# A planner of issue order is given a later landing time for the memory tokens of layer 0 and a longer duration for one product

## The chip, the cores and the metric

The kernel runs on one core of a Trainium2 chip. The metric is the device time of one execution, in microseconds (us). The core's engines run at the same time, each through its own queue in program order: PE (TensorE, matrix products and transposes), ACT (ScalarE), DVE (VectorE), POOL (GpSimd) and SP (SyncE, which here only issues DMAs).

## The reference

The reference is a decoder trunk of two layers on S = 256 tokens of width D = 1024, in float32. A layer runs three token-mixing branches on the same normed input, merges them, and then runs an MLP:

```
h = rmsnorm(x, ln_mix_pre[l])
xr, yr, q, kv, g_nsa, qm, g_merge = split(h @ w_in[l])
o_a = rglru_branch(xr, yr, ...)                # conv, gates, scan
o_b = nsa_branch(q, kv, g_nsa, positions, ...) # compressed, selected, window attention
o_c = memory_branch(qm, mem, ln_mem[l], w_mem_kv[l])  # rmsnorm(mem) @ w_kv, 4 heads
ga, gb, gc = split(sigmoid(g_merge))
merged = ga*(o_a @ w_br_rnn) + gb*(o_b @ w_br_nsa) + gc*(o_c @ w_br_mem)
x = x + rmsnorm(merged @ w_out[l], ln_mix_post[l])
h = rmsnorm(x, ln_mlp_pre[l])
x = x + rmsnorm(square(relu(h @ mlp_w1[l])) @ mlp_w2[l], ln_mlp_post[l])
```

The compressed part of `nsa_branch` (`compress`) builds overlapping blocks of 32 tokens from the keys and values, adds a position table, and sends them through a small MLP with a gelu.

## The kernel before

**Products.** Every weight matrix comes in units of 512 KB (usually two slices of 128 rows by 512 columns). SP loads a unit into one of five `raw` buffers (`dma_unit`, L336 to L343). ACT copies it to `whi` in the format that PE multiplies (a unit of 128x1024), and DVE subtracts to get the remainder `wlo` (`split_unit`, L345 to L364); there are four pairs of these. Activations are kept as such a pair too (`hTh` and `hTl`, and so on), and PE makes each product of three passes: high by high, high by low, low by high. A unit is 24 products of 256 columns, or 12 of 512.

**The order.** The issue order is not written by hand. While the program is built, `Meter` (L109 to L140) meets every call of an engine, works out a cost for it from the shapes, and advances a clock of that engine in `Order` (`od.T`, L78 to L93). Each strand of dependent work is a generator, a `Lane`, with `r`, the planned time at which its last result is there. `side` and `step` (L255 to L295) put the next piece of a lane into the order when its planned time has come on PE's planned clock. So a price in `Meter.call` or a planned landing does nothing on the chip by itself: it moves instructions ahead of others in the queues of PE, ACT, DVE and POOL, and where SP issues for a lane, in SP's. The chip then runs each queue in that order. In the profile all computing instructions carry the line of `Meter.call`, L140.

**The memory tokens.** `mem_prep` (L1751) loads the 256 memory tokens (four tiles of 128x512, L1760) behind the gains of their norm (L387), and spawns `norm_both`: for each of two token tiles, ACT squares and sums both halves (`junk<-mem`), POOL makes `rstd`, DVE scales each half (`hn<-mem,rstd,gain`), PE transposes it (`tr<-ident,hn`), and ACT and DVE copy it into the pair `mTh` and `mTl`. In `norm_both`, the first piece of each lane is allowed at `od.cur.r`, which `mem_prep` sets. For layer 0 it is called when the first job starts (`start`), for layer 1 at a later job. PE's first job in layer 0 is `xr1` and the second `xr0`, each 96 products of four units; units are counted here u0, u1, ... from the first.

**The compressed keys.** `kc_epi` (L1477) copies the product's result with ACT (`kcs<-mm`, two of them), and SP copies each of these with four DMAs into two shifted tiles (`g<-kcs`, L1489 and L1490). DVE then adds the position table (`gs<-g,pet`), ACT and DVE split the sum (`ghl`), and PE multiplies it (`hid`). Around it, ACT and DVE serve the recurrent branch: PE makes the gate products `gp`, ACT turns them into `ti`, `tr`, `aa`, `th`, and so on.

**The end of the mixing sub-layer.** `Residual` (L537) sums squares of the last product `wo`, adds the result to `x`, norms it and transposes it (`tr<-ident,hn`) for the MLP, one token tile after the other; products of `wo` for the second tile stand before and behind the first tile's transposes.

Of the kernel before, what the change touches and what calls it, by code (L numbers as in the profile page):

```python
# [11 lines left out]
F32 = mybir.dt.float32  # L12
# [86 lines left out]
def elems(ap):  # L99
    n = 1  # L100
    for d in ap.shape[1:]:
        n *= d
    return n


class Meter:
# [5 lines left out]
    def __getattr__(self, name):  # L112
        fn, key, order = getattr(self.eng, name), self.key, self.order

        def call(*args, **kw):
            out = kw["out"] if "out" in kw else args[0]
            n = elems(out)
            if key == "A":
                cost = 0.055 + n / 1200.0
                cost += 0.06 * sum(not isinstance(kw.get(k, 0.0), float) for k in ("scale", "bias"))  # L120
                cost += 0.12 if kw.get("accum_out") is not None else 0.0
                if args[2] in TABLES:
                    cost += 1.28 * (self.table != TABLES[args[2]])
                    self.table = TABLES[args[2]]
            elif key == "D":
                if "reduce" in name:
                    n = elems(args[1])
                cost = DCOST + n / (1920.0 if name == "tensor_scalar" else 960.0)
                cost += 0.06 * (name == "scalar_tensor_tensor")
            elif key == "P":  # L130
                if name == "transpose":
                    cost = 0.109
                else:
                    load = args[1].shape[1] / 1200.0
                    cost = max(load, 0.0025 + n / 2400.0) * (4 if args[1].dtype == F32 else 1)
            else:
                cost = 0.25
            aps = [v.tensor.name for v in (*args, *kw.values()) if hasattr(v, "tensor")]
            order.note(key, cost, out.tensor.name, aps if "out" in kw else aps[1:])
            return fn(*args, **kw)  # L140

        return call
# [3 lines left out]
def trunk_kernel(ctx, tc, x, mem, positions, ln_mix_pre, w_in, conv_w, conv_b, lru_wr, lru_br, lru_wi, lru_bi,  # L146
# [3 lines left out]
    od = Order()  # L150
# [22 lines left out]
    def a(shape, dt=F32, name="a"):  # L173
        return sp.tile(shape, dt, tag="a", bufs=NA, name=nm(name))
# [39 lines left out]
    def spawn(gen, name=None, prio=None, child=None):  # L214

        ln = Lane(gen, od.cur.r, od.cur.child if prio is None else prio)
        ln.child = child or od.cur.child
        ln.last = od.cur.last
        lanes.append(ln)
        lanes.sort(key=lambda v: v.prio)  # L220
        if name:
            named[name] = ln
        advance(ln)
        return ln
# [110 lines left out]
    dma_clock = [0.0]  # L335
# [47 lines left out]
    def gain_tile(g):  # L383
        res = []
        for h in range(2):
            gt = a([P, 512], F32, name="gain")
            nc.sync.dma_start(out=gt, in_=g[:, 512 * h:512 * h + 512].to_broadcast([P, 512]))  # L387
            res.append(gt)
        return res
# [126 lines left out]
    def norm_both(src, gt, o, name, prio=1):  # L516
        yield [spawn(norm_lane(src[t], t, gt, o, name), prio=prio) for t in range(NT)]
# [1235 lines left out]
    def mem_prep(l):  # L1753
        ms = []
        gm = gain_tile(ln_mem[l:l + 1, :])
        for t in range(NT):
            ms.append([])
            for h in range(2):
                m = a([P, 512], F32, "mem")
                nc.sync.dma_start(out=m, in_=mem[0, t * P:(t + 1) * P, 512 * h:512 * h + 512])  # L1760
                ms[t].append(m)
        env[l]["M"] = XT("mT")
        dma_clock[0] = max(dma_clock[0], od.T["D"] - 4.0) + 6 * 0.73
        od.cur.r = max(od.cur.r, dma_clock[0] + 2.0)
        spawn(norm_both(ms, gm, env[l]["M"], f"mnorm{l}"))

    def load_x(t):
# [9 lines left out]
    for l in range(DEPTH):  # L1777
        layer(l)
    jobs[0]["gb1"].pre = lambda: mem_prep(1)
    order = []  # L1780
    for l, names in enumerate((ORDER0, ORDER1)):
# [14 lines left out]
    def start():  # L1796
        first_pre()
        mem_prep(0)
        prows = load_params()
        load_consts()  # L1800
        od.cur.r = 26.0
        spawn(prm_lane(prows), "prm")
        od.cur.r = 36.0
        spawn(const_lane(), "const")
# [35 lines left out]
```

## Time and profile before

| | before |
|---|---|
| median of 3 runs | 1221.04 us (1216.6, 1221.04, 1221.95) |
| the profiled execution, its own time | 1221.59 us |
| its span in the trace | 1219.9 us |
| PE busy | 1199.6 us, 98% |
| DVE busy | 901.6 us, 74% |
| ACT busy | 736.7 us, 60% |
| POOL busy | 35.5 us, 3% |
| HBM traffic | 208.16 MB read, 172 GB/s over the span |

The profile is of one execution, 0.55 us above the median of the runs. The busy time of PE is that of pipelined instructions: a product of 256 columns is shown 0.28 us long while the next starts 0.12 us behind it, so gaps between starts say more than busy shares. The waits are rows of the timeline in which an idle time stands in brackets, with the engine and tile that ended it.

### The profile page before, as it was taken

The numbers are of one execution on the slowest core, as the hardware profiler recorded it, in microseconds if no ns is written. First come the engines' busy times: TensorE is split into PE (matmuls) and PEld (weight loads), VectorE is DVE, ScalarE is ACT, GpSimd is POOL, SyncE is SP. The second block draws the span as 40 slices with busy tenths as digits, with TensorE's granted clock in tenths as the row PEclk, the third lists the DMA queues.
The fourth block names the chain that finished last, engine by engine and source line by source line (L and its number), as shares of the span: only waits on it lengthen the run. The fifth ranks groups of instructions, "written<-read, shape, count | busy, mean of one in ns | idle before, by whom it ended". The sixth has DMA issues, their size and how long they took to land.

```text
span 1219.9 us, 19570 instructions
## 1 busy us (share of the span) xinstructions
PE 1199.6 (98%) x7371; PEld 1068.8 (88%) x7371; DVE 901.6 (74%) x1516; ACT 736.7 (60%) x1330; POOL 35.5 (3%) x88
## 2 busy tenths in 40 slices
PE   8899999999999999999999999999999999999997
PEld 7899988888888889998989999888888887899896
DVE  4778897979898686555557587998978877655555
ACT  4677856777666465445456688675656655645443
POOL 3000000000000020000001000000000001000000
PEclk9899999999999999999999999999999999999999
DMA  8555656753345666666656556584534356565561
GB/s 283 181 161 168 190 156 181 223 152 108 122 131 186 233 191 191 194 189 189 206 174 210 154 171 176 153 258 140 154 121 138 121 164 217 166 187 183 190 190 69
DMA packets 121263, 212.58 MB, mean 174 GB/s; under 512 B 10441, under 2 KB 24098, under 8 KB 121169
## 3 DMA queue, kind: packets, MB, share of 16 engines
q1 hardware_dynamic: 120752, 211.19, 55.9%
q8 instruction: 58, 0.95, 0.3%
q0 software_dynamic: 416, 0.15, 0.1%
q14 instruction: 37, 0.30, 0.1%
HBM read 208.16 MB, written 1.05 MB: 172 GB/s over the span
## 4 chain that ended last, share of the span: by engine, by line
PE 92%; DVE 2%; DMA 2%; ACT 2%; issue 1%; SPq 0%; POOL 0%; POOLq 0%; DVEq 0%; ACTq 0%
PE mm L140 62%; PE acc L140 14%; PE ob L140 2%; PE sc L140 2%; PE wo L140 2%; PE pt L140 2%; PE hid L140 1%; PE gp L140 1%; PE mo L140 1%; PE msc L140 1%; PE tr L140 1%; DMA mem<-in_mem_dram 1%; ACT junk L140 1%; DVE wlo L140 1%; DMA raw<-in_mlp_w_dram 1%
## 5 line engine op out<-in xcount | busy, mean ns | idle before, releaser
L140 DVE TENSOR_TENSOR wlo<-raw,whi 128x1024 fp32r<-128x1024 f32 (+1 forms) x371 | 447.1, 1214 | 225.7 <-ACT whi L140 224.3
L140 ACT ACTIVATE whi<-raw 128x1024 fp32r<-128x1024 f32 (+1 forms) x371 | 385.3, 1055 | 204.9 <-PE mm L140 117.0
L140 PE MATMUL mm<-hmh,whi 128*128 128x256 f32 x480 | 135.9, 283 | 0.0
L140 PE MATMUL mm<-hmh,wlo 128*128 128x256 f32 x480 | 135.9, 283 | 0.0
L140 PE MATMUL mm<-hml,whi 128*128 128x256 f32 x480 | 135.9, 283 | 0.0
L140 PE MATMUL mm<-hTh,whi 128*128 128x256 f32 x448 | 129.4, 289 | 0.0
L140 PE MATMUL mm<-whi,hTh 128*128 128x512 f32 x320 | 129.1, 403 | 0.0
L140 PE MATMUL mm<-hTh,wlo 128*128 128x256 f32 x448 | 127.6, 285 | 0.0
L140 PE MATMUL mm<-hTl,whi 128*128 128x256 f32 x448 | 127.6, 285 | 0.0
L140 PE MATMUL mm<-wlo,hTh 128*128 128x512 f32 x320 | 125.1, 391 | 0.0
L140 PE MATMUL mm<-whi,hTl 128*128 128x512 f32 x320 | 125.0, 391 | 0.0
L140 PE MATMUL acc<-whi,rh 128*128 128x512 f32 x256 | 99.8, 390 | 0.0
L140 PE MATMUL acc<-wlo,rh 128*128 128x512 f32 x256 | 99.8, 390 | 0.0
L140 PE MATMUL acc<-whi,rl 128*128 128x512 f32 x256 | 99.6, 389 | 0.0
L140 PEld LDWEIGHTS mm<-hmh,whi 128*128 128x128 f32 x480 | 92.1, 192 | 0.5
L140 PEld LDWEIGHTS mm<-hml,whi 128*128 128x128 f32 x480 | 92.1, 192 | 0.5
L140 PEld LDWEIGHTS mm<-hmh,wlo 128*128 128x128 f32 x480 | 92.1, 192 | 0.0
L140 PEld LDWEIGHTS mm<-hTh,whi 128*128 128x128 f32 x448 | 86.9, 194 | 0.2
L140 PEld LDWEIGHTS mm<-hTl,whi 128*128 128x128 f32 x448 | 86.9, 194 | 0.2
L140 PEld LDWEIGHTS mm<-hTh,wlo 128*128 128x128 f32 x448 | 86.7, 194 | 0.0
L140 PEld LDWEIGHTS mm<-whi,hTl 128*128 128x128 f32 x320 | 60.1, 188 | 13.1
L140 PEld LDWEIGHTS mm<-whi,hTh 128*128 128x128 f32 x320 | 60.2, 188 | 12.0 <-issue 0.2
(311 smaller groups left out, 2467.7 us busy)
## 6 DMA issues: line engine op xcount, KB each, us to landing
raw<-in_w_in_dram SPq DMA_DIRECT2D x136, 512.0 KB, 3.7
raw<-in_mlp_w_dram SPq DMA_DIRECT2D x128, 512.0 KB, 4.2
raw<-in_w_mem_kv_dram SPq DMA_DIRECT2D x32, 512.0 KB, 4.2
raw<-in_cmp_w_dram SPq DMA_DIRECT2D x16, 512.0 KB, 4.0
raw<-in_w_br_rnn_dram SPq DMA_DIRECT2D x16, 512.0 KB, 3.7
raw<-in_w_br_mem_dram SPq DMA_DIRECT2D x16, 512.0 KB, 3.7
raw<-in_w_br_nsa_dram SPq DMA_DIRECT2D x16, 512.0 KB, 3.7
raw<-in_w_out_dram SPq DMA_DIRECT2D x16, 512.0 KB, 4.5
```

The costliest lines, as they stand in the source:

```text
L140: return fn(*args, **kw)
```

## The change

Two expressions of the planner differ. In `Meter.call`, a product of n columns that is not plain float32 is priced at 0.0133 + n/2400 us instead of 0.0025 + n/2400: 0.120 us instead of 0.109 for 256 columns, and 0.227 instead of 0.216 for 512. A plain float32 product, of which there are few, is priced at four times 0.001 + n/2400. In `mem_prep`, the memory tokens of layer 0 are planned to land 12 us behind the planner's DMA clock instead of 2; for layer 1 it stays 2.

```diff
@@ -132,7 +132,7 @@
                     cost = 0.109
                 else:
                     load = args[1].shape[1] / 1200.0
-                    cost = max(load, 0.0025 + n / 2400.0) * (4 if args[1].dtype == F32 else 1)
+                    cost = (max(load, 0.0133 + n / 2400.0) if args[1].dtype != F32 else 4 * max(load, 0.001 + n / 2400.0))
             else:
                 cost = 0.25
@@ -1761,7 +1761,7 @@
         env[l]["M"] = XT("mT")
         dma_clock[0] = max(dma_clock[0], od.T["D"] - 4.0) + 6 * 0.73
-        od.cur.r = max(od.cur.r, dma_clock[0] + 2.0)
+        od.cur.r = max(od.cur.r, dma_clock[0] + (2.0 if l else 12.0))
         spawn(norm_both(ms, gm, env[l]["M"], f"mnorm{l}"))
```

PE's queue holds the same instructions as before, in another order. A few scalings and copies that either ACT or DVE may do go to the other of the two: ACT's queue has 15 instructions fewer and DVE's 15 more. SP's queue has one difference, in layer 0, where the eight DMAs of `g<-kcs` stand behind one more `raw`; POOL's is the same. Three places follow, with the names as the program numbers them.

**Place 1, layer 0, the memory tokens on PE.** Products of `xr0` around the first transposes; `whi_374` is u5, `whi_426` is u6 before, `whi_473` is u7 now, and `pet` is the transpose of the position table. Before, and now:

```order
L140 MATMUL mm_437<-hTh_114,whi_374 128x256
L140 MATMUL mm_437<-hTl_115,whi_374 128x256
L140 MATMUL mm_437<-hTh_114,wlo_375 128x256
L140 MATMUL tr_515<-ident,hn_456 128x128 x4
L140 MATMUL mm_436<-hTh_116,whi_426 128x256
```

```order
L140 MATMUL mm_417<-hTl_119,whi_473 128x256
L140 MATMUL mm_417<-hTh_118,wlo_474 128x256
L140 MATMUL pet_606<-ident,per_103 128x128
L140 MATMUL tr_621<-ident,hn_560 128x128 x4
L140 MATMUL tr_626<-ident,hn_562 128x128 x4
L140 MATMUL mm_646<-hTh_112,whi_512 128x256
```

The first transposes have moved from behind u5 to behind u7 and `pet`, 48 products later, and both halves of the first token tile now stand together; the second tile's two follow behind 12 products.

The same place on ACT, whose rows `junk<-mem` wait for the memory tokens; `raw_220` is u6, `raw_312` u7, `raw_318` u8. Before, and now:

```order
L140 ACTIVATE whi_374<-raw_214 128x1024
L140 ACTIVATE junk_392,ss_393<-mem_230 128x512
L140 ACTIVATE junk_395,ss_396<-mem_232 128x512
L140 ACTIVATE junk_398,ss_399<-mem_234 128x512
L140 ACTIVATE junk_401,ss_402<-mem_236 128x512
L140 ACTIVATE xs_416<-mm_263 128x512
L140 ACTIVATE xs_417<-mm_264 128x512
L140 ACTIVATE whi_426<-raw_220 128x1024
L140 ACTIVATE whi_485<-raw_312 128x1024
L140 ACTIVATE sp_476<-sp_475 128x16
L140 ACTIVATE whi_530<-raw_318 128x1024
```

```order
L140 ACTIVATE whi_374<-raw_214 128x1024
L140 ACTIVATE whi_406<-raw_220 128x1024
L140 ACTIVATE xs_404<-mm_263 128x512
L140 ACTIVATE xs_405<-mm_264 128x512
L140 ACTIVATE sp_450<-sp_449 128x16
L140 ACTIVATE whi_473<-raw_312 128x1024
L140 ACTIVATE whi_512<-raw_318 128x1024
L140 ACTIVATE junk_542,ss_543<-mem_230 128x512
L140 ACTIVATE junk_545,ss_546<-mem_232 128x512
L140 ACTIVATE junk_548,ss_549<-mem_234 128x512
L140 ACTIVATE junk_551,ss_552<-mem_236 128x512
L140 ACTIVATE whi_564<-raw_348 128x1024
```

The copies of u6, u7 and u8, and the two `xs`, stood behind the four rows of the memory tokens, and stand ahead of them now.

**Place 2, layer 1, the compressed keys.** ACT, from the gate product's `ti` on. Before, and now:

```order
L140 ACTIVATE ti_8284<-gp_8344,hb 128x256 x2
L140 ACTIVATE kcs_8360<-mm_8176 128x512
L140 ACTIVATE kcs_8361<-mm_8177 128x512
L140 ACTIVATE tr_8283<-gp_8364,hb 128x256 x2
L140 ACTIVATE aa_8285<-tr_8283,cc 128x256 x2
L140 ACTIVATE th_8286<-tr_8283,cc 128x256 x2
L140 ACTIVATE tr_8283<-aa_8285 128x512
L140 ACTIVATE ti_8323<-gp_8367,hb 128x256 x2
```

```order
L140 ACTIVATE ti_8254<-gp_8314,hb 128x256 x2
L140 ACTIVATE tr_8253<-gp_8332,hb 128x256 x2
L140 ACTIVATE aa_8255<-tr_8253,cc 128x256 x2
L140 ACTIVATE th_8256<-tr_8253,cc 128x256 x2
L140 ACTIVATE tr_8253<-aa_8255 128x512
L140 ACTIVATE ti_8293<-gp_8335,hb 128x256 x2
L140 ACTIVATE gelu_8195<-gelu_8195 128x512
L140 ACTIVATE whi_8349<-raw_8102 128x1024
L140 ACTIVATE kcs_8379<-mm_8222 128x512
L140 ACTIVATE kcs_8380<-mm_8223 128x512
L140 ACTIVATE whi_8399<-raw_8136 128x1024
```

The rows `kcs<-mm` stood right behind the first `ti`; now `tr`, `aa`, `th`, `tr`, the other `ti`, a gelu and a `whi` stand ahead of them. In PE's queue the `gp` products of that `tr` stand 24 products earlier than before, and the products of the next units where they stood.

DVE, from the end of the first group of `gs` to the second, which waits for the later four copies `g`. Before, and now:

```order
L140 TENSOR_TENSOR gs_8378<-g_1656_8373,pet 128x8x15
L140 TENSOR_TENSOR wlo_8436<-raw_8168,whi_8435 128x1024
L140 SCALAR_TENSOR_TENSOR gelu_8195<-gelu_8195,ys_8161 128x512
L140 MEMSET gs_8386 128x32
L140 TENSOR_TENSOR gs_8386<-g_1658_8380,pet 128x8x15
```

```order
L140 TENSOR_TENSOR gs_8388<-g_1656_8383,pet 128x8x15
L140 MEMSET gs_8396 128x32
L140 TENSOR_TENSOR gs_8396<-g_1658_8390,pet 128x8x15
L140 TENSOR_TENSOR gs_8396<-g_1659_8391,pet 128x8x15
L140 TENSOR_TENSOR gs_8396<-g_1658_8390,pet 128x8x15
L140 TENSOR_TENSOR gs_8396<-g_1659_8391,pet 128x8x15
L140 TENSOR_TENSOR wlo_8455<-raw_8214,whi_8454 128x1024
```

A `wlo` and a gelu stood between the two groups of `gs`; now both groups stand together, ahead of that `wlo`. Behind that `wlo` DVE's queue now holds `ghl`, `ti`, `th`, `wlo`, `ghl`, `gs`, `wlo`, as before in the same sequence; then `ghl`, `ml`, `ghl`, `ti`, two `xc`, a gelu and a `wlo`, where it had a `wlo` behind the first of its `ml`, `ghl`, `ti` and `th`.

**Place 3, layer 1, the transposes behind `wo` on PE.** Before, and now:

```order
L140 MATMUL wo_11286<-we_11376,mgl_11169 128x512
L140 MATMUL wo_11286<-we_11377,mgh_11168 128x512
L140 MATMUL wo_11286<-we_11379,mgh_11168 128x512
L140 MATMUL wo_11286<-we_11377,mgl_11169 128x512
L140 MATMUL tr_11522<-ident,hn_11512 128x128 x4
L140 MATMUL tr_11527<-ident,hn_11514 128x128 x4
L140 MATMUL wo_11287<-we_11392,mgh_11168 128x512
```

```order
L140 MATMUL wo_11286<-we_11376,mgh_11168 128x512
L140 MATMUL wo_11286<-we_11378,mgh_11168 128x512
L140 MATMUL wo_11286<-we_11376,mgl_11169 128x512
L140 MATMUL tr_11519<-ident,hn_11512 128x128 x4
L140 MATMUL tr_11524<-ident,hn_11514 128x128 x4
L140 MATMUL wo_11286<-we_11377,mgh_11168 128x512
L140 MATMUL wo_11286<-we_11379,mgh_11168 128x512
```

The two transposes of the first token tile stand three products of 512 columns earlier.

## Rows read from the trace of the kernel before

**Rows 1.** The page, busy time of the engines: share of the span, instructions.
```profile
PE 1199.6 (98%) x7371; PEld 1068.8 (88%) x7371; DVE 901.6 (74%) x1516; ACT 736.7 (60%) x1330; POOL 35.5 (3%) x88
```

**Rows 2.** Timeline of PE: start, duration, instruction, in brackets the idle time before.
```profile
31.53 0.28 PE L140 MATMUL mm<-hTh,wlo 128*128 128x256 f32 x1
34.97 1.12 PE L140 MATMUL tr<-ident,hn 128*128 128x128 f32 x4 [3.16 <-DVE hn L140]
...
41.26 0.28 PE L140 MATMUL mm<-hTh,wlo 128*128 128x256 f32 x1
41.38 1.04 PE L140 MATMUL tr<-ident,hn 128*128 128x128 f32 x8
42.17 0.36 PE L140 MATMUL mm<-hTh,whi 128*128 128x256 f32 x1
```

**Rows 3.** Table by stretch: busy of each engine, granted clock, DMA share, GB/s.
```profile
35.00:40.60 5.60, 5.60 (x27) 5.60 (x28) 5.39 (x14) 2.36 (x6) 0.00 (x0) 0.50 0.93 272
...
1026.00:1029.00 3.00, 1.36 (x8) 0.86 (x7) 1.23 (x3) 1.57 (x6) 1.76 (x4) 1.00 0.82 279
```

**Rows 4.** Timeline of ACT around the memory tokens.
```profile
28.34 0.63 ACT L140 ACTIVATE junk<-mem 128x512 bf16<-128x512 f32 x1 [7.17 <-DMA mem<-in_mem_dram]
...
29.01 0.63 ACT L140 ACTIVATE junk<-mem 128x512 bf16<-128x512 f32 x1
...
31.95 2.00 ACT L140 ACTIVATE whi<-raw 128x1024 fp32r<-128x1024 f32 x2
```

**Rows 5.** Timeline of POOL there, the first tile's `rstd`.
```profile
30.15 0.57 POOL L140 TENSOR_TENSOR rstd<-var,mhalf 128x1 f32<-128x1 f32 x1
```

**Rows 6.** The load of u8: its issue, and the time to its landing.
```profile
L341 SPq DMA_DIRECT2D raw<-in_w_in_dram x1: 379/379/379, 24.6 to 24.6; - x1
...
DMA to landing us min/median/max: 8.4/8.4/8.4
```

**Rows 7.** Timeline of ACT in layer 1.
```profile
740.88 1.30 ACT L140 ACTIVATE kcs<-mm 128x512 f32<-128x512 f32 x2
742.45 0.84 ACT L140 ACTIVATE tr<-gp,hb 128x256 f32<-128x256 f32 x2 [0.27 <-PE gp L140]
...
747.05 2.00 ACT L140 ACTIVATE whi<-raw 128x1024 fp32r<-128x1024 f32 x2
```

**Rows 8.** Timeline of SP there, the last issue of the compressed keys.
```profile
746.02 0.62 SPq L1490 DMA_DIRECT2D g<-kcs  x1
```

**Rows 9.** Tile g in layer 1: time from issue to landing.
```profile
DMA to landing us min/median/max: 3.0/3.5/3.9
```

**Rows 10.** Timeline of DVE in layer 1.
```profile
754.84 0.42 DVE L140 TENSOR_TENSOR ghl<-gs,ghl 128x256 fp32r<-128x256 f32 x1
...
758.13 0.90 DVE L140 TENSOR_TENSOR gs<-g,pet 128x120 f32<-128x120 f32 x3
758.95 1.22 DVE L140 TENSOR_TENSOR wlo<-raw,whi 128x1024 fp32r<-128x1024 f32 x1
760.08 0.68 DVE L140 TENSOR_TENSOR ml<-mm,mh 128x512 fp32r<-128x512 f32 x1
...
769.58 0.69 DVE L140 SCALAR_TENSOR_TENSOR ti<-th,ti 128x512 f32<-128x512 f32 x1
...
772.22 1.22 DVE L140 TENSOR_TENSOR wlo<-raw,whi 128x1024 fp32r<-128x1024 f32 x1
```

**Rows 11.** Timeline of PE, where it first reads the `wlo` behind the second group.
```profile
752.85 0.28 PE L140 MATMUL mm<-hTh,wlo 128*128 128x256 f32 x1
```

**Rows 12.** Timeline of PE around the first tile's transposes behind wo, layer 1.
```profile
1026.23 0.62 PE L140 MATMUL wo<-we,mgh 128*128 128x512 f32 x2
1026.68 0.39 PE L140 MATMUL wo<-we,mgl 128*128 128x512 f32 x1
1028.71 1.32 PE L140 MATMUL tr<-ident,hn 128*128 128x128 f32 x8 [1.64 <-DVE hn L140]
```

**Rows 13.** Waits of PE from 45 us on: for whom, total, times, longest.
```profile
PE gn L140 <- DVE wlo L140: 0.9, 1, 0.9
```

## The prediction

> **What bounds the kernel now.** The page's first part comes first: PE is busy for 1199.6 us [rows 1], so time is gained or lost only where PE stands or runs slowly. Hence I read PE's timeline for starts that lie further apart than the pitch, 0.12 us for a product of 256 columns (41.26 to 41.38), 0.225 for one of 512 (two in 0.45 us), 0.10 for a transpose (eight in 0.79) [rows 2, 12], and looked up what each gap waited for.
>
> The largest is the memory tokens' in layer 0. ACT stood 7.17 us for them until 28.34, with the copy of u6 queued behind: that starts at 31.95 [rows 4]. DVE has u6's `wlo` in its queue ahead of `hn`, so the first transposes, which wait for `hn`, start at 34.97, 3.3 us after PE was done with the product of 31.53 [rows 2]. Then PE runs at a granted clock of 0.50, the 1.2 GHz level, from 35.0 to 40.6 [rows 3]. In all, 31.53 to 42.17 is 10.64 us [rows 2] for 25 products and 16 transposes, 25 x 0.12 + 16 x 0.10 = 4.6. The price of this stall is **6.0 us**: 3.3 standing and 2.7 of slow clock.
>
> A shorter wait shows no such tail: before the transposes behind `wo` in layer 1 PE stood from 1026.9 to 1028.71 [rows 12], and the granted clock of that stretch is 1.00 [rows 3].
>
> **Part 1: the memory tokens (the later landing).** The transposes come 48 products and `pet` later in PE's queue: 31.65 + 48 x 0.12 + 0.1 = 37.5. Are they ready? On ACT the copies of u6, u7 and u8 now stand ahead of `junk<-mem`. u8 was issued at 24.6 and took 8.4 us to land [rows 6]: 33.0, when the tokens have landed, since ACT's rows for them ran on from 28.34 [rows 4]. Its copy takes about 0.95 (the second of a pair that starts at 31.95 and is 2.00 long [rows 4]), so `junk` starts at 33.95. Its rows are 0.67 apart [rows 4], so the first tile's two end at 35.3. From the end of those two in the trace (29.01 + 0.67) to that of `rstd` (30.15 + 0.57) is 1.0 [rows 4, 5]: 36.3. The two `hn` are taken at 0.7 each, as DVE's `ti` of the same shape (0.69 [rows 10]): done at 37.0 and 37.7. PE wants them at 37.5 and 37.9. The second tile is 1.35 later on both sides. So this just fits; I leave 0.3 us of waiting. Gain: **-6.0 + 0.3 = -5.7**. What hides ACT's work here is PE's 48 products; where u8 lands later, the cover is gone (a rival, below). The DMAs of the tokens do not move in SP's queue.
>
> **Part 2: the price of a product.** On PE itself the order is free: same instructions, about as many changes between kinds of product, taken at nothing (an estimate; bounds half a microsecond either way, four pitches). What the new price takes away is a cushion. The planner thought a unit of 24 products took 24 x 0.109 = 2.6 us; it takes 2.9. So everything it placed n units ahead of its use had 0.26 x n us to spare on the chip, and in the new order it has none. The trace's pitch of 0.12 [rows 2] is the new price, and that is why I count the cushion as gone. The Trainium skill, "TensorE: Matmul & The Clock Gate", Back-to-back issue gap, gives n/2.4 GHz + 2.5 ns for a lone warm product, 0.109 us for 256 columns, which is the price of before. By it PE would be faster than the new plan, the cushions would not matter, and only Part 1 would be left of the sum; the trace does not bear it out for this stream.
>
> I followed the new order at the durations of the trace for places where ACT or DVE now come late.
>
> The worst is **layer 1's compressed keys**. Their `gp` and `tr` come 24 products earlier, so `tr` starts at 742.45 - 2.9 = 739.6. Behind it stand `tr` to gelu, which before took 747.05 - 742.45 = 4.6 [rows 7], and a `whi` of 0.95: `kcs` starts at 745.1, not 740.88 [rows 7], 4.25 later. SP's eight issues follow it. The last moves from 746.02 [rows 8] to 750.25 and lands 3.0 to 3.9 us later, median 3.5 [rows 9]: 753.75. DVE, whose queue is in order, cannot pass the `gs` that need it. Three of them take 0.82 (758.13 to 758.95), the `wlo` behind is done 1.22 later [rows 10]: 755.8. PE wants that `wlo` at 752.85 [rows 11]; before, the `wlo` stood ahead of the second group. PE waits **3.0 us** (2.5 and 3.4 at the ends of the landing time). Behind it on DVE comes a sequence that the trace has from 754.84 to 760.08, 5.24 us, then `ghl`, `ml`, `ghl` (0.4 + 0.6 + 0.4, durations of 0.42 and 0.68 less the overlap with the next), then `ti` to `wlo` (769.58 to 772.22, and 1.22, so 3.9) [rows 10]: from 755.7 on that is 10.5, so the third `wlo` after is done at 766.2. PE gets there after 22 products of 256 columns and 25 of 512, 8.3 us after 755.85: 764.2. It waits **2.0** more.
>
> In the place of the **transposes behind wo** nothing on the chain to `hn` moves, but three products of 0.225 that lay inside the wait now lie behind it [rows 12]: **+0.7** (nothing, if the second tile's wait has the same to spare; 0.7 at most).
>
> **Eight smaller places** of the same kind remain, most with a `wlo` that comes late: the largest in layer 0's `hid`, about 1.0, where rotary products and three small pieces now stand ahead of it on DVE, the rest 0.1 to 0.5. No row shows them. Below they are bounded by nothing, above by eight waits like that for `gn`'s `wlo`, 0.9 [rows 13], so 7. I take **2.5**, a third, since a cushion of one unit is 0.26. Scalings that go from ACT to DVE cost nothing: they stand in front of no late `wlo`.
>
> **The sum.** -5.7 + 3.0 + 2.0 + 0.7 + 2.5 = +2.5. The profiled execution took 1221.6, so 1224.1; it lies 0.55 above the median of the runs, so **1223.5** against that.
>
> **Rivals.**
> - *The cushions do not matter, faster.* Part 1's gain comes, and part 2's waits are hidden, because DVE and ACT are further ahead of PE than my walk from row to row has them. For it: DVE is busy for only 901.6 us [rows 1]. Against: at the compressed keys it is a transfer, not DVE's load, that comes late. 1221.6 - 5.7 = 1215.9, against the median 1215.3. Chance 0.20; in about half of it a wait of before (as that for `gn`) goes too, which is what takes it past 0.5%.
> - *The memory wait stays, slower.* ACT's queue now holds `junk` behind u8's copy, and u8 shares its landing with the tokens'. Loads there took 8.4 us [rows 6]. If u8 takes 2 us more (landing past 35), PE stands 2 us or more at 37.5 and the clock falls to its 1.2 GHz level as it did behind 3.3 us: 2.0 + 2.7 instead of 0.3 is +4.4, so 1228.5, against the median 1227.9. It decides from a wait somewhere between 1.8 (clock kept) and 3.3 us (fell). Chance 0.10.
> - *The clock falls at the new waits.* 3.0 us at the compressed keys is nearer to 3.3 than to 1.8. The slow clock costs 2.7, but gives DVE time for its 2.0: +0.7. At the transposes behind `wo` the wait is 2.5; falling there adds 2.7. Together 1224.1 + 3.4 = 1227.5, against the median 1227.0. Chance 0.15.
> - *The change does not do what it says.* The order shows the transposes moved, so only a landing of the tokens later than u8 would undo it. 0.02, priced as the memory wait.
>
> **Numbers.** The forecast has 0.53. Its own range is 1220 to 1227: below, the small places at nothing (-2.5) and 0.5 each for the landing of `g` and for PE's changes of product; above, the same 1.0 and the small places half-way to their upper bound (+2.3). The first rival ends at 1215.3 and the memory wait at 1227.9; with both taken in, the range is 1215 to 1228.5, and under 2 in 10 are left outside. A measurement of this kernel can tell about 0.5% from no change, 6.1 us: under 1214.9 or over 1227.1. Faster: half of the first rival, 0.10, and 0.02 from the forecast's lower end. Slower: the memory wait 0.10, half of the clock's case 0.07, and the last rival 0.02, together 0.19. The same: 0.69.
>
> **What would show it.** In the changed kernel's trace: PE's wait for the memory tokens' `hn` under 0.5 us and a granted clock near 1.00 at 35 to 41 us; around 750 us a wait of PE for `wlo` of 2.5 to 3.4 and one of about 2.0 some 8 us later; the wait before the transposes behind `wo` at 2.5 instead of 1.8. The prediction is wrong if the first is not gone, or if the second pair is missing; if the pair is there with a clock of 0.50 behind it, the third rival holds.

## The result, and the profile after

The changed kernel takes 1238.22 us (median of 6 runs, 1236.4 to 1239.79) against 1219.29 for the kernel before (6 runs, 1215.06 to 1221.95): a ratio of 1.0157, 95% interval 1.0133 to 1.0181, some 19 us slower. The forecast was 1223.5, no change, with a range of 1215 to 1228.5; the result lies far above it.

The busy line of the page, which answers to [rows 1], shows what the span of 1234.4 us already says: the same instructions, and PE still busy for all but a little.

```profile
PE 1206.3 (98%) x7371; PEld 1069.5 (87%) x7371; DVE 906.7 (73%) x1531; ACT 732.6 (59%) x1315; POOL 40.4 (3%) x88
```

The profiled execution took 1236.4 us, 14.8 more than that of before. It is the fastest of its six runs, 1.8 under their median, and that of before lies 2.3 above the median of the six beside it, so the two profiles show 14.8 of the 19 us. To see where, I went through PE's timeline and took, for every start, the distance to the next start less the pitch (0.120 us for a product of 256 columns, 0.227 for 512, 0.109 for the rest), and summed this by stretch. The column in the middle is a second trace of the kernel before, of an execution of 1218.72 us; it comes up below.

| stretch, us | before, first trace | before, second trace | after |
|---|---|---|---|
| 0 to 50 | 13.0 | 8.4 | 6.3 |
| 50 to 150 | 3.6 | 3.6 | 8.8 |
| 150 to 350 | 2.6 | 2.8 | 7.6 |
| 350 to 700 | 2.0 | 2.4 | 2.9 |
| 700 to 850 | 3.7 | 3.4 | 12.0 |
| 850 to 1000 | 3.6 | 3.5 | 4.8 |
| 1000 to the end | 4.5 | 6.2 | 5.4 |

**The memory tokens** behave as worked out. In PE's timeline of the changed kernel, the eight transposes that answer to those of [rows 2] follow `pet` without a wait, and the table by stretch has the full clock where [rows 3] had 0.50 (columns as there):

```profile
36.68 0.27 PE L140 MATMUL pet<-ident,per 128*128 128x128 f32 x1
36.79 1.04 PE L140 MATMUL tr<-ident,hn 128*128 128x128 f32 x8
37.58 0.37 PE L140 MATMUL mm<-hTh,whi 128*128 128x256 f32 x1
```

```profile
35.00:41.00 6.00, 6.00 (x54) 6.00 (x53) 5.79 (x16) 4.57 (x12) 0.93 (x1) 1.00 0.67 209
```

They had more room than was worked out, and that is luck: u8 landed at 29.45 here and at 32.97 in the first trace of before, so ACT's first `junk`, right behind u8's copy, starts at 30.52 instead of 33.95. Whether the transposes would still come without a wait behind a landing as late as that, this trace does not show.

```profile
29.55 1.06 ACT L140 ACTIVATE whi<-raw 128x1024 fp32r<-128x1024 f32 x1 [0.31 <-DMA raw<-in_w_in_dram]
30.52 0.61 ACT L140 ACTIVATE junk<-mem 128x512 bf16<-128x512 f32 x1
```

**The compressed keys of layer 1.** The predicted wait is there, longer, and with half a clock behind it. PE's timeline, and the two stretches:

```profile
758.18 0.28 PE L140 MATMUL mm<-hTl,whi 128*128 128x256 f32 x1
762.23 0.58 PE L140 MATMUL mm<-hTh,wlo 128*128 128x256 f32 x1 [3.77 <-DVE wlo L140]
762.61 0.41 PE L140 MATMUL mm<-hTh,whi 128*128 128x256 f32 x1
```

```profile
757.00:762.00 5.00, 1.46 (x13) 1.26 (x11) 3.49 (x10) 2.28 (x5) 0.00 (x0) 0.90 0.77 205
762.00:768.00 6.00, 5.77 (x25) 5.63 (x26) 6.00 (x14) 5.13 (x8) 0.00 (x0) 0.51 0.60 176
```

DVE's timeline shows the queue: three times `gs` waits for a copy `g`, and only then comes the `wlo` for which PE stands.

```profile
757.14 0.37 DVE L140 TENSOR_TENSOR gs<-g,pet 128x120 f32<-128x120 f32 x1 [2.19 <-DMA g<-kcs]
758.14 0.88 DVE L140 TENSOR_TENSOR gs<-g,pet 128x120 f32<-128x120 f32 x3 [0.64 <-DMA g<-kcs]
...
759.08 0.35 DVE L140 TENSOR_TENSOR gs<-g,pet 128x120 f32<-128x120 f32 x1
760.17 0.88 DVE L140 TENSOR_TENSOR gs<-g,pet 128x120 f32<-128x120 f32 x3 [0.74 <-DMA g<-kcs]
760.96 1.22 DVE L140 TENSOR_TENSOR wlo<-raw,whi 128x1024 fp32r<-128x1024 f32 x1
```

SP's timeline and ACT's show why the copies are late. ACT is done with the first `kcs` some 0.6 us behind 750.58, but SP stands in three `raw` loads from 742.34 to 752.34, the last of which waits for a free buffer (DVE's `wlo` of 750.72 has read it at 751.95), and issues the first copy behind them.

```profile
742.34 10.00 SPq L341 DMA_DIRECT2D raw<-in_w_in_dram  x3
752.43 0.49 SPq L1489 DMA_DIRECT2D g<-kcs  x1
...
756.95 0.62 SPq L1490 DMA_DIRECT2D g<-kcs  x1
```

```profile
749.63 1.05 ACT L140 ACTIVATE whi<-raw 128x1024 fp32r<-128x1024 f32 x1
750.58 1.08 ACT L140 ACTIVATE kcs<-mm 128x512 f32<-128x512 f32 x2
```

**Many more waits for `wlo`.** The list of PE's waits from 45 us on, which answers to [rows 13]; in the kernel before, `mm` waited 0.2 us in all for a `wlo`:

```profile
PE mm L140 <- DVE wlo L140: 8.3, 7, 3.8
...
PE pt L140 <- DVE pl L140: 1.5, 1, 1.5
PE hid L140 <- DVE wlo L140: 0.8, 1, 0.8
PE mm L140 <- DVE rt L140: 0.7, 1, 0.7
PE gn L140 <- DVE wlo L140: 0.5, 1, 0.5
```

The largest of them, beside the keys', is in layer 0: PE stands at 136.6, and the clock falls again.

```profile
136.62 0.39 PE L140 MATMUL mm<-whi,mTh 128*128 128x512 f32 x1
138.80 0.50 PE L140 MATMUL mm<-wlo,mTh 128*128 128x512 f32 x1 [1.79 <-DVE wlo L140]
139.14 0.40 PE L140 MATMUL mm<-whi,mTl 128*128 128x512 f32 x1
```

```profile
137.00:139.00 2.00, 0.21 (x2) 0.20 (x2) 2.00 (x3) 1.35 (x2) 0.00 (x0) 1.00 0.00 0
139.00:144.00 5.00, 5.00 (x16) 3.94 (x16) 5.00 (x8) 2.26 (x5) 0.00 (x0) 0.66 0.78 222
```

On DVE there is no gap from 126.64 to 141: softmax, scan, gelu, the second `gs`, a remainder and another scan stand ahead of the two `wlo` of 137.53. In the kernel before, DVE stood idle for 3.29 us before the corresponding `wlo`, until its `whi` was there.

```profile
126.64 0.61 DVE L140 TENSOR_SCALAR mp<-mp,msm 128x256 f32<-128x256 f32 x2
...
127.89 1.27 DVE L140 TENSOR_TENSOR_SCAN xc<-aa,ti 128x256 f32<-128x256 f32 x2
...
134.30 0.68 DVE L140 TENSOR_TENSOR oal<-gelu,oah 128x512 fp32r<-128x512 f32 x1
134.90 0.68 DVE L140 SCALAR_TENSOR_TENSOR ti<-th,ti 128x512 f32<-128x512 f32 x1
135.61 1.27 DVE L140 TENSOR_TENSOR_SCAN xc<-aa,ti 128x256 f32<-128x256 f32 x2
136.92 0.69 DVE L140 SCALAR_TENSOR_TENSOR gelu<-xc,gelu 128x512 f32<-128x512 f32 x1
137.53 2.35 DVE L140 TENSOR_TENSOR wlo<-raw,whi 128x1024 fp32r<-128x1024 f32 x2
```

```profile
135.27 1.22 DVE L140 TENSOR_TENSOR wlo<-raw,whi 128x1024 fp32r<-128x1024 f32 x1 [3.29 <-ACT whi L140]
```

DVE's queue does not make all of these waits. Of the seven waits of `mm` in the list it makes two, the keys' and this one, 5.6 of the 8.3 us. In the other five (behind 76.1, 124.1, 238.1, 316.2 and 924.8, 2.8 us in all) DVE stands idle until ACT has made the `whi`, and ACT, without a gap before it, is late itself: here behind eight `qs`. From PE's timeline, DVE's and ACT's:

```profile
239.37 0.50 PE L140 MATMUL mm<-wlo,hTh 128*128 128x512 f32 x1 [0.76 <-DVE wlo L140]
238.09 1.23 DVE L140 TENSOR_TENSOR wlo<-raw,whi 128x1024 fp32r<-128x1024 f32 x1 [4.58 <-ACT whi L140]
233.87 3.11 ACT L140 ACTIVATE qs<-qtr 64x256 fp32r<-64x256 f32 x8 [1.52 <-PE qtr L140]
237.00 2.01 ACT L140 ACTIVATE whi<-raw 128x1024 fp32r<-128x1024 f32 x2
```

### The profile page after: what moved, and what is told of

The parts are those of the page before. It is cut to its first block, busy times and chain, and to the rows that moved or that the text cites. A ratio compares the mean times of both kernels' runs of the same rounds, so it can differ in the third digit from the quotient of the medians.

```text
span 1234.4 us, 19597 instructions
## 1 busy us (share of the span) xinstructions
PE 1206.3 (98%) x7371; PEld 1069.5 (87%) x7371; DVE 906.7 (73%) x1531; ACT 732.6 (59%) x1315; POOL 40.4 (3%) x88
## 4 chain that ended last, share of the span: by engine, by line
PE 83%; DVE 7%; ACT 5%; issue 2%; DMA 1%; POOL 1%; SPq 0%; DVEq 0%; POOLq 0%; ACTq 0%
PE mm L140 55%; PE acc L140 14%; DVE wlo L140 2%; PE sc L140 2%; PE ob L140 2%; PE wo L140 2%; PE pt L140 1%; ACT whi L140 1%; PE mo L140 1%; PE msc L140 1%; PE gp L140 1%; PE tr L140 1%; PE hid L140 1%; ACT junk L140 1%; DVE rt L140 1%
## 5 line engine op out<-in xcount | busy, mean ns | idle before, releaser
L140 ACT ACTIVATE pr<-sc,mx 128x256 f32<-128x256 f32 (+1 forms) x128 | 52.1, 428 | 38.8 <-DVE mx L140 38.7
L140 PEld LDWEIGHTS mm<-wlo,hTh 128*128 128x128 f32 x320 | 60.4, 189 | 13.4 <-DVE wlo L140 3.5
```

## The experiments

In what follows, theory A is that the new price takes away a cushion and the later landing is a gain; theory E is its sharper form, that the *ratio* of the engines' prices sets how much ACT and DVE work the plan packs in front of a `wlo`. Each is a few characters in the planner; no experiment leaves out any part of the computation. "Waits for wlo" is the sum of the lines of that releaser in the list of PE's waits. Each batch has its own runs of the kernel before beside it (medians 1217.3, 1219.0, 1218.2 and 1217.6), and the ratios are to those.

### One half of the change at a time

```diff
-cost = (max(load, 0.0133 + n / 2400.0) if args[1].dtype != F32 else ...)
+cost = max(load, 0.0025 + n / 2400.0) * (4 if args[1].dtype == F32 else 1)
```

> Only the later landing of the memory tokens; the price of a product stays as before. Theory A (the new price takes the cushion away, the later landing is a plain gain): the stall at the memory tokens is gone (the changed kernel's trace shows -6.7 us there), a new wait or two of 0.5 to 1.0 us appears in the memory branch's keys and values near 80 us, so 1213 to 1216 us, 3 to 6 under before; no wait of over 0.5 us around 750 us. Rival B (it is the later landing that pushes later jobs into each other): most of the 19 us are here too, 1230 us or more.

Measured: 1219.55 us, ratio 1.0019 (1.0008 to 1.0029). It is not the landing that costs 19 us, so rival B falls; but theory A's gain of 3 to 6 us is not there either. In its trace the tokens' stall is gone, and three new waits stand in its place: 1.7 us for a `wlo` at 37.6, 0.7 for a `whi` and 0.9 for its `wlo` at 84 and 85, and the wait before the transposes behind `wo`, whose order is unchanged, is 2.38 us of idle instead of 1.64 [rows 12] (1.90 in the second trace of before), with a clock of 0.66 behind it:

```profile
1024.37 0.39 PE L140 MATMUL wo<-we,mgl 128*128 128x512 f32 x1
1027.13 1.22 PE L140 MATMUL tr<-ident,hn 128*128 128x128 f32 x5 [2.38 <-DVE hn L140]
```

```profile
1026.00:1030.00 4.00, 2.87 (x11) 2.60 (x12) 3.05 (x6) 1.32 (x4) 1.08 (x2) 0.66 0.20 76
```

```diff
-        od.cur.r = max(od.cur.r, dma_clock[0] + (2.0 if l else 12.0))
+        od.cur.r = max(od.cur.r, dma_clock[0] + 2.0)
```

> Only the new price of a product; the landing of the memory tokens stays as before. Theory A: the stall at the memory tokens is back (+5 to +7 against the changed kernel) and the new waits stay, the one of 3.9 us around 758 us among them: 1243 to 1246 us. Rival B: the new waits go, 1215 to 1222 us.

Measured: 1240.08 us, ratio 1.0178 (1.0159 to 1.0197). The price by itself makes all of the loss. The later landing is worth some 2 us on top of it, not 5 to 7, and the intervals of the two ratios overlap, so that even the 2 us are not shown. In this trace the stall at the tokens is back with 1.9 us (30.61 to 32.63, less a pitch), at the full clock.

### More and less of the price

The same line with other constants; the last three of these came in a later batch, and the first two of those have the landing at 6 instead of 12.

> The changed kernel with a price half-way, 0.0079 + n/2400 (0.1146 us for 256 columns), between the old 0.109 and the measured 0.120. Theory A in its plain form (the lost cushion is in proportion to the price): half of the new waits' 21 us, so about 1224 us. Theory A with a threshold (waits come only once the cushion is below what ACT and DVE are late by): 1213 to 1217 us, like the later landing alone. Rival C (every new order has its own accidental waits, whatever the price): anywhere between 1213 and 1240.

> The changed kernel with a price above the measured one, 0.0240 + n/2400 (0.131 us for 256 columns). Theory A: the plan now has PE later than it is, ACT and DVE come later still for it, and the waits grow beyond the changed kernel's: 1243 us or more. Rival C: no trend, 1225 to 1240 us, above or below the changed kernel. Rival D (a longer price gives DVE and ACT more room in the plan, so waits go): under 1230 us.

> A price of 0.0050 + n/2400 (0.112 us for 256 columns), with the tokens' landing at 6. Theory E (the waits for wlo grow with the price): between the old price (1219) and 0.0079 (1227): 1219 to 1224 us, PE's waits for wlo between 3 and 6 us. Rival C (each order has its own accidents, the trend seen so far is luck): anywhere from 1213 to 1235.

> A price of n/2400 alone (0.107 us for 256 columns), below the old 0.109, with the tokens' landing at 6. Theory E one-sided (a cheaper product always gives more cushion): at or below the old price's time, 1214 to 1219 us, waits for wlo under 2 us. Theory E two-sided (work held back in the plan comes late at the ends of the attention branches): waits for wlo under 2 us, but new waits at the ends of attention, 1220 to 1228 us.

> A price of n/2400 - 0.0080 (0.099 us for 256 columns), with the landing at 12 as in the changed kernel. Theory E two-sided: few waits for wlo, but waits of 1 to 3 us each at the ends of the attention branches (near 385 and 985 us) and before products that need the rotated keys: 1225 to 1240 us. Theory E one-sided: 1214 to 1220 us.

| price, + n/2400 | median, us | ratio to before | waits for wlo, us |
|---|---|---|---|
| -0.0080 | 1238.38 | 1.0170 (1.0138 to 1.0203) | 3.5 |
| 0 (landing 6) | 1236.18 | 1.0157 (1.0118 to 1.0195) | 2.9 |
| 0.0025 (old; landing 12) | 1219.55 | 1.0019 (1.0008 to 1.0029) | 3.3 |
| 0.0050 (landing 6) | 1224.49 | 1.0060 (1.0039 to 1.0081) | 2.4 |
| 0.0079 | 1226.98 | 1.0068 (1.0052 to 1.0083) | 5.6 |
| 0.0133 (the change) | 1238.22 | 1.0157 (1.0133 to 1.0181) | 9.6 |
| 0.0240 | 1248.36 | 1.0245 (1.0228 to 1.0262) | 12.1 |

Above the old price time rises with every step, and so, from 0.0079 on, do the waits for `wlo`. Half of the price's step brings 7.4 of the 18.7 us: somewhat less than half, near the plain form of theory A (it had 1224 us), and not its form with a threshold (1213 to 1217). Rival D falls. The 0.0050 came out just above theory E's time and below its 3 to 6 us of waits for `wlo`. Below the old price the time rises as well, at once and by as much, with few waits for `wlo` but others: at a price of 0, `mm` waits 4.0 us for a `whi`, and `ob`, `pt` and products wait for the attention's pieces near 400 and 1000 us. So the one-sided form of theory E falls, and the time rises to both sides of the old price. The price of 0 is also beyond the two-sided form's 1220 to 1228, and that 0 and 0.0025 lie 17 us apart is no smooth slope: I take part of it for rival C, an order's own accidents, which no run separates from the price. The 0.0050 has one too, a wait of 2.7 us for `mTl`.

### Is it the price or the ratio?

```diff
+            cost *= 0.91 if key in "AD" else 1.0
             aps = [v.tensor.name for v in (*args, *kw.values()) if hasattr(v, "tensor")]
```

with the old price of a product, and `1.1` in place of `0.91` with the new one.

> PE's price as before, the later landing, and every price of ACT and DVE times 0.91: the same ratio between the engines' prices as in the changed kernel, without its new price of a product. Theory E (ratio: a unit of 24 products in the plan holds as much ACT and DVE work as the ratio allows; where it is filled to the brim, DVE's small work stands ahead of the next wlo and PE waits for it): slow like the changed kernel, 1232 to 1243 us, and PE's waits for wlo sum to 5 us or more, against 0.2 in the kernel before and 8.3 in the changed one. Theory F (it is the absolute price of a product that does it, by the times at which lanes are let in): 1217 to 1222 us, like the later landing alone.

> The changed kernel with every price of ACT and DVE times 1.1: the old ratio again, at the new price of a product. Theory E: PE's waits for wlo fall from 8.3 us to under 3, the wait of 3.9 us around 758 us goes, the time falls below the changed kernel's 1238; how far is open, since the fixed times in the plan (landings, hand-overs, the 3 us of look-ahead) are not scaled, and work that the plan holds back can come late at the end of the attention branches (380 to 395 us, 980 to 995 us): 1218 to 1232 us. Theory F: no better than the changed kernel, 1236 us or more, with the waits for wlo still there.

Measured: 1246.03 us, ratio 1.0224 (1.0201 to 1.0248), for the changed ratio at the old price; its list of PE's waits (L141 there, as the edit adds a line):

```profile
PE mm L141 <- DVE wlo L141: 5.7, 9, 0.9
PE hid L141 <- DVE wlo L141: 3.3, 2, 2.5
```

F falls, and E holds in kind (the waits for `wlo` sum to 9.0 us; the time lies above its 1243): the price of a product need not be touched to make the kernel as slow as the change does, or slower. With the ratio restored: 1243.33 us, 1.0199 (1.0177 to 1.0222). The waits for `wlo` go from 9.6 to 4.1 (the main kind, for `mm`, from 8.3 to 1.6), which is the way that theory E says, but the time, for which it had 1218 to 1232, does not follow. So the ratio is shown to move the waits for `wlo`; that it sets the time is not shown. The plan's fixed times were not scaled with the prices, and no run scales them all together. The waits have moved to the ends of the attention branches, the longest here:

```profile
1006.40 0.58 PE L141 MATMUL ob<-pl,vx 128*128 128x256 f32 x1 [4.48 <-DVE pl L141]
```

The same, one engine at a time (`"D"` and `"A"` in place of `"AD"`, times 1.1):

> The changed kernel with DVE's prices alone times 1.1. Theory E-DVE (DVE's queue, filled to the brim, makes the waits for wlo): the waits for wlo fall as with both engines dearer (from 8.3 to under 3 us), and the late ends of attention near 385 and 985 us appear as there: 1238 to 1248 us. Theory E-ACT (it is ACT's whi): the waits for wlo stay at 6 us or more.

> The changed kernel with ACT's prices alone times 1.1, which is near ACT's measured pitch (0.95 to 0.98 us for a whi that the plan prices at 0.908). Theory E-DVE: the waits for wlo stay, 5 us or more, 1234 to 1246 us. Theory E-ACT (with PE's price true, ACT's was the only one left too low, so the plan is true now): the waits go and the time falls to 1218 to 1225 us.

DVE alone: 1245.69 us, 1.0218 (1.0198 to 1.0239); the waits for `wlo` fall from 9.6 to 1.2 us (0.3 for `mm`), and the waits at the ends of attention are there, at 386 to 402 us and from 993 us. ACT alone, whose price this brings near to what a trace shows: 1234.68 us, 1.0128 (1.0104 to 1.0151), with 5.3 us of waits for `wlo` left, 4.4 of them for `mm`. So DVE's price against PE's weighs most in the waits for `wlo`, and ACT's takes nearly half of them away too; and with the prices of all three engines nearest to the traces the kernel is still 16 us behind the one with the old set.

### The queue of the compressed keys, and the look-ahead

```diff
-            od.cur.r += 3.0
+            od.cur.r += 5.0
             yield spawn(blocks_lane(l, j, g2, E["gx"]), prio=0.5)
```

> The changed kernel with the compressed keys' copies planned to land 5 us after their issue instead of 3 (both layers). If the wait around 758 us comes from DVE standing in its queue for those copies, ahead of a wlo, it shrinks from 3.9 to under 1 us and the half clock behind it goes: -4 to -6 us by itself, 1232 to 1235 us, less what other waits this new order brings (up to +3). If it comes from DVE's load alone, it stays at 3 us or more and the time at 1237 to 1240.

Measured: 1236.5 us, 1.0145 (1.012 to 1.0171), 2 us under the change, though the intervals of the two ratios overlap. The wait of 3.9 us and the half clock behind it are gone; near that place PE now waits once for 1.12 us (idle), just over the expected 1, then for 0.7 and 1.3, and for 2.2 before `hid` at 806.5, behind which the granted clock is 0.51 from 809 to 812.5.

```profile
762.52 0.50 PE L140 MATMUL mm<-wlo,hTh 128*128 128x512 f32 x1 [1.12 <-DVE wlo L140]
```

So the copies did block the `wlo`; but DVE's work was not less for it, and most of the wait came back further on: by the sums of the table, the stretch from 700 to 850 us has 11.1 us instead of 12.0.

```diff
-    HORIZON, TOL, AHEAD = 3.0, 0.07, 3
+    HORIZON, TOL, AHEAD = 1.0, 0.07, 3
```

> The changed kernel with the planner's look-ahead cut from 3 us to 1: work of ACT and DVE is let into their queues only up to 1 us ahead of PE's planned clock. Theory E (work let in ahead of a wlo makes PE wait for it): the waits for wlo fall from 8.3 us to under 4; the ends of attention may come later. If the waits for wlo do not fall, the backlog is not made by the look-ahead but by the order of arrival. Time 1225 to 1245 us.

Measured: 1250.97 us, 1.0259 (1.0237 to 1.0281), the slowest median of all and above the expected 1245. No wait of `mm` for a `wlo` is among its longer ones, only one of `hid` (2.5): holding the small work back does take it from in front of `wlo`. The price is again at the other end:

```profile
PE mm L140 <- DVE obl L140: 4.1, 4, 1.2
PE gp L140 <- DVE xc L140: 3.1, 1, 3.1
PE hid L140 <- DVE wlo L140: 2.5, 1, 2.5
```

### The stall of before, and a landing between

> The kernel before, once more, for a second trace of it: its profiled execution of 1221.6 us lies 4 us above the median that many runs have since given (1217.3). If the stall at the memory tokens varies, this trace shows it shorter than 3.3 us of standing or without the stretch at half clock, and the rest of the program alike.

Its trace is of 1218.72 us. The same program, the same order, but the tokens land 2.0 us earlier relative to [rows 4] (ACT's first `junk` starts at 26.34, not 28.34), and PE stands for 0.64 us of idle and keeps its clock:

```profile
32.08 0.28 PE L140 MATMUL mm<-hTh,wlo 128*128 128x256 f32 x1
32.99 0.66 PE L140 MATMUL tr<-ident,hn 128*128 128x128 f32 x4 [0.64 <-DVE hn L140]
33.41 0.36 PE L140 MATMUL mm<-hTh,whi 128*128 128x256 f32 x1
```

```profile
33.00:36.00 3.00, 3.00 (x26) 3.00 (x27) 2.93 (x7) 2.15 (x6) 0.00 (x0) 1.00 0.87 241
```

So the stall of 6.0 us is not what this kernel has in each execution: here it is 0.8 (32.08 to 32.99, less a pitch). The rest is alike but for the transposes behind `wo`, where the clock fell in this trace (0.66 from 1024 to 1029) and not in the first.

```diff
-        od.cur.r = max(od.cur.r, dma_clock[0] + (2.0 if l else 12.0))
+        od.cur.r = max(od.cur.r, dma_clock[0] + (2.0 if l else 6.0))
```

with the old price.

> The price of a product as before, and the memory tokens of layer 0 planned to land 6 us behind the planner's DMA clock instead of 2 or 12. The order puts the tokens' squares on ACT behind u6's copy and ahead of u7's, and the first transposes 36 products later than before. Theory A for the landing (only what waits for the tokens should move behind them): no wait of PE for the tokens' hn, and no wait of 0.7 us or more for a wlo near 37 and 85 us, as the landing at 12 had; against the kernel before, whose stall was 0.8 us in one trace and 3.3 us with half clock in another, 1 to 4 us less: 1214 to 1218 us. Rival (what is gained early is given back at the transposes behind wo in layer 1, where the first loads of the MLP set the time): within 1 us of the kernel before.

Measured: 1219.25 us, ratio 1.0 (0.9989 to 1.0012). No wait of PE for the tokens' `hn` is left, but waits of 0.6 and 0.8 us for a `whi` and its `wlo` come at 88 and 89 us, and the transposes behind `wo` wait 2.2 us instead of 1.8 (2.06 in the second trace of before). The rival's time holds, its place does not: against the second trace, by the sums of the table, this order gains 1.7 us in the first 50 us and loses 2.2 from 50 to 150. It is the best order with a changed line, and no better than the kernel before.

## Why the prediction was wrong

**What bounds the kernel** was right: only PE's waits and its clock matter, and 14.5 of the 14.8 us between the two profiles are found there, the whole difference of their spans. Of the **rivals** only the third came, and in part: the clock fell at the keys, not at the transposes behind `wo`. None reached the size of the loss.

**Part 1, the memory tokens: -5.7.** The mechanism is shown step by step: the transposes run at 36.79 without a wait, at the full clock, and the first 50 us are 6.7 us shorter than in the first trace. The price was of one execution. In the second trace the stall is 0.8 us and the first 50 us are only 2.1 longer than in the changed kernel; with the landing alone, the time does not fall. So the term was too large for the runs: with the new price they make it some -2, not clear of the noise, and with the old price the kernel was 2 us slower with the later landing than without (1219.55 and 1217.28). The forecast took its base from an execution with a stall that the second trace does not have, and the gain with it.

**Part 2, the compressed keys: 3.0 + 2.0.** Right in place and kind. `kcs` starts 7.7 us ahead of PE's product in the changed trace (750.58 and 758.30), as worked out (745.1 and 752.85). The wait is 3.9 instead of 3.0, because "SP's eight issues follow it" left out that SP's queue is in order too: a `raw` that waited for its buffer held the first copy until 752.43, 1.2 us more than before between `kcs` and its first copy (741.50 - 740.88 = 0.6, now 1.85). The second wait of 2.0 is not there; in its place the clock fell (0.51 from 762 to 768), for 2.6 us, as the third rival said. Together 6.5 instead of 5.0.

**The transposes behind wo: +0.7.** Against the first trace the stretch from 1000 us on is 0.9 longer; against the second it is 0.8 shorter, since there, with the order of before, PE stood 2.06 us and the clock fell. The wait itself is 2.1 us, where the forecast had 2.5 instead of 1.8. The term is smaller than what one execution differs by from the next.

**Eight smaller places: 2.5.** This is the step that failed. In the changed trace there are not eight but fifteen places of 0.3 to 2.0 us between 50 and 1000 us, 13 us in all with the half clock behind the one at 136.6 (the order before had 2.3 us of such places); in the table, the stretches from 50 to 700 and from 850 to 1000 are 12 us longer than in either trace of before, and some 2 of the stretch from 700 to 850 are theirs. That is 14 us against the forecast's 2.5; what the places do not hold of it lies in gaps of under 0.25 us each. The upper bound of 7 was too low as well: it multiplied the number of places that the walk had found by the largest wait of the kernel before, and both factors were taken from an order that has few such waits. The places are not independent: DVE's queue is filled over a dozen microseconds, as from 126.64 to 141, and a `wlo` at its end is late by the sum. And the walk's "most with a `wlo` that comes late" does not say which engine is late: in five of the seven waits of `mm` it is ACT.

**Why a cushion** was right in kind: the price alone makes the loss. The experiments put it better for the waits for `wlo`, where it is the ratio of PE's price to the others', DVE's above all. My reading of it, worked out from the planner's prices and shown by no run, is this: with the old price the plan counted a unit of 24 products as 2.62 us and a `wlo` as 1.14, which left DVE 1.5 us for small work in each unit; with the new one it leaves 1.74, and fills them. On the chip the small pieces also wait for ACT and for copies, as the traces show. The rule of the Trainium skill ("TensorE: Matmul & The Clock Gate", Back-to-back issue gap: n/2.4 GHz + 2.5 ns for a lone warm product) did not describe this stream: the changed kernel's products follow each other at 0.12 us too (36.32, 36.44, 36.56 in its timeline), and the rival that it led to did not come.

**What stays open.** Why the old price, with the rest of the planner's constants, gives the best order of those tried is not shown. That the time rises to both sides is; but 17 us between a price of 0 and of 0.0025 is more than a slope explains, and I have not found which early choice makes it. One rival was not tested: the twelve experiments that move a price, the look-ahead or the keys' landing are all slower than the kernel before, whichever way they move it, and that would also be so if its order were merely an unusually good one.

## What to carry to other kernels

In a scheduler like this one, a cost is a lever on the order and not a statement about the chip: making one engine's price true while the others stay as they are changes the ratio, and with it how much work is packed in front of what the bounding engine needs next. When a change re-orders a whole program, count the places where it could now wait over the whole of it and let them add up, before the two or three that can be worked out are priced. And the largest stall of a profile is to be looked up in a second profile of the same kernel, before its removal is counted.

## What the runs showed of the hardware

The landing of the same loads in the same program differed by 2.0 us between two executions (28.34 and 26.34), and with it a stall by a factor of four (3.3 and 0.8 us) and the clock behind it (0.50 and 1.00). The clock behind waits of about 2 us goes either way, so the forecast's limit between 1.8 and 3.3 us does not hold: the granted clock was 1.00 after 1.80 us of standing [rows 12] and after 2.11 in the changed kernel at 1039.9 to 1042.2, and fell behind 1.95 (0.66 from 139 to 144, a mean over a stretch that is at the 1.2 GHz level, 0.50, from 139.8 to 143.2) and behind 2.06 in the second trace of before. A copy within the chip's memory was 3.3 to 4.1 us on its way here, but a further 1.2 us passed before SP could issue it, behind a load that had to wait for its buffer.
